# Softmax attention in a hybrid encoder block: sine products of the queries on GpSimd, half of the probabilities' products on ScalarE, and the values split during the linear attention

## The chip, the cores and the metric

The kernel runs on one core of one Trainium2 chip. The metric is device time in microseconds (us), the median of several executions. A core has five engines that run their own instruction lists in order and meet at semaphores: TensorE (PE in the profile: matmuls and transposes into PSUM), VectorE (DVE), ScalarE (ACT), GpSimd (POOL) and SyncE (SP), which in this kernel issues every DMA.

## The reference, cut to what matters

One encoder layer over 1024 tokens of width 1024: a projection of the normalized input, a gated linear attention (GLA), a softmax attention over a window of +-128 tokens (SWA), their gated sum, and a SwiGLU network. The part that the change touches is the softmax attention, with 8 query heads, 2 key/value heads, a head width of 128 and blocks of 128 tokens:

```python
def _rope(x, pos):
    ...
    x1, x2 = x[..., :half], x[..., half:]
    return jnp.concatenate([x1 * cos - x2 * sin, x2 * cos + x1 * sin], axis=-1)

def _swa_branch(q, k, v, q_g, k_g, sinks):
    ...
    q = _rope(_rms_norm(q.astype(f32).reshape(bsz, s, SWA_HEADS, hd), q_g), pos)
    k = _rope(_rms_norm(k.astype(f32).reshape(bsz, s, hkv, hd), k_g), pos)
    ...
    scores = jnp.einsum("bnqhgd,bnkhd->bnhgqk", qb, kc) * (hd ** -0.5)
    ...
    m = jnp.maximum(scores.max(axis=-1, keepdims=True), sink)
    p = jnp.exp(scores - m)
    denom = p.sum(axis=-1, keepdims=True) + jnp.exp(sink - m)
    o = jnp.einsum("bnhgqk,bnkhd->bnqhgd", p / denom, vc)
```

The probabilities, divided by their sum, multiply the values of up to three neighbouring blocks. All is float32.

## The kernel before, in words

Matrix products keep float32 accuracy by three passes: each operand is split into a rounded high part (type fp32r; names ending in h) and the remainder (names ending in l), and `mm3` runs high x high, high x low and low x high into the same PSUM tile. A weight unit of 128x512 is loaded by SP into one of 4 buffers `wr` (L68), rounded by ACT into `wh` (L70) and subtracted by DVE into `wl` (L72).

PE's order is written by hand: in the stages of the two attentions, `slot` calls small functions of the attention (called stages here) and, between them, `fill` takes dense matmuls (tiles `mm`) of the projections that are still due from the list `dense`. So while PE waits for an attention step it cannot reorder; a wait of PE there is lost unless a later wait becomes shorter by it. The other engines' orders are set by the scheduler that builds the program: it simulates the program with its own costs and lists each engine's instructions in the order in which they came to be ready there. It also gives out the buffers of pools in that order: the four PSUM banks for the attention's tiles (`ch`), and the SBUF buffers of each tag.

The GLA stage comes first (linear attention, functions `g_*`, 4 heads x 8 chunks of 128 tokens). For each chunk `g_scores` loads the split values `vh`, `vl` (3 buffers each in the pool `gt`), `g_out` reads them, and `g_turn` transposes the output (PE, L771), copies it with ACT into `ot` (L773) and stores it (L775, `o<-ot`). At the end of the stage stand 8 calls of `k_norm(t)`: each loads a block of keys of the softmax attention (`kvr`), normalizes and rotates it, and stores it to DRAM (`key`). They are called in the last slots, but all engines except PE run them as early as their data and buffers allow. The dense work beside the stage's end is the last of the projection to `sq1` (`proj_t`: PSUM tiles copied by ACT at L186, stored at L187, `sq<-st`) and the first of `r0`, `r1` (`proj_f`).

`glas.close()` frees the pools of the GLA stage. The buffers of the softmax attention (SWA) lie in the same memory, so its first loads (`cosb`, `sinb`, `band`, `qg`, `sink`) wait for the last users of those buffers. From these tables DVE builds `qA` and `qB` (L859 to L862), which hold the cosine and sine times the key-side gain.

The SWA stage treats 16 chunks: 2 groups g of 4 heads, by 8 blocks n of 128 queries. Chunk i is loaded (`a_load`) in slot i, prepared in slot i+1 (`a_prep`: `qr` squared by ACT, summed by DVE; the rotation is two products with `qB` at L912 and L914, one with `qA` at L916, and a sum at L917), transposed in slot i+2 (`a_turn`), scored in slot i+3 (`a_scores`: for each of four heads three matmuls into a `ch` bank, then DVE's row maximum `mx` at L941; behind the fourth head the maxima with the sink, four exponentials on ACT at L956, their sums `dn`, the reciprocal `rd` at L960 and four products of the probabilities `p` with `rd` on POOL at L962), and finished in slot i+5 (`a_probs`: PE transposes the probabilities by key block, ACT rounds them to `ph` at L976, DVE makes `pl` at L977; `a_out`: products with the split values). In the slots of the first 8 chunks `k_load(t)` loads a block of keys and of values, `k_turn` transposes the keys (`kTh`, `kTl`), and `k_prep` splits the values: `vSh` on ACT (L894), `vSl` on DVE (L895).

## Time and profile before

| | before |
|---|---|
| median of 3 runs | 1645.5 us (1644.73 to 1645.68) |
| the profiled execution, its own time | 1645.61 us |
| its span in the profile | 1643.8 us |
| granted TensorE clock in the span | 1.00 |
| busy in the span: PE, DVE, ACT, POOL | 1626.0, 1251.4, 842.6, 76.0 us |
| DMA moved | 262.91 MB |

Busy PE time is the union of the matmuls' modelled times, so it counts as busy what runs behind each other without a gap; PE's idle time is the span less that. Line numbers (L912) are those of the kernel before. A row of the timeline gives the start in us, the length in us, the engine, the line, the operation, the tiles as out<-in, the shapes and, in square brackets, how long the engine had been idle and what released it. SPq is SP's queue of DMA issues.

### The profile page before, as it was taken

What the parts mean: (1) busy time and instruction counts of PE and PEld (TensorE: products, weight loads), DVE (VectorE), ACT (ScalarE), POOL (GpSimd) and SP (SyncE); (2) the same over time, 40 slices, a digit from 0 to 9 for tenths busy, and PEclk for the clock granted to TensorE, in tenths of its full rate; (3) what the DMA queues carried; (4) which work ended last, traced back from release to release, by engine and by line L of the source; (5) the groups of instructions that cost most, each with busy time, mean ns of one, the idle gap of its engine ahead of it and who ended that gap; (6) DMA issues with size and microseconds to landing.
All of it is one profiled execution on the core that took longest, in us unless ns stands there. A gap on an engine that the chain in (4) does not pass through costs nothing.

```text
span 1643.8 us, 23281 instructions
## 1 busy us (share of the span) xinstructions
PE 1626.0 (99%) x7588; PEld 1346.0 (82%) x7588; DVE 1251.4 (76%) x2559; ACT 842.6 (51%) x1762; POOL 76.0 (5%) x68
## 2 busy tenths in 40 slices
PE   9999999999999989999999999999999999999999
PEld 7888888888888778888888888888888888888887
DVE  8866665589986598867885678887777778779655
ACT  8622224468998666665554557333333333354442
POOL 0000000000000034540000000000000000000000
PEclk9999999999999999999999999999999999999999
DMA  7554334475554633248765544443334443596433
GB/s 238 176 178 148 115 122 135 173 250 173 179 161 129 191 108 97 77 138 280 225 205 175 168 146 145 140 149 109 109 115 147 142 147 129 177 341 193 149 98 119
DMA packets 168010, 262.91 MB, mean 160 GB/s; under 512 B 19324, under 2 KB 52860, under 8 KB 167888
## 3 DMA queue, kind: packets, MB, share of 16 engines
q1 hardware_dynamic: 167888, 261.42, 49.8%
q8 instruction: 60, 0.98, 0.2%
q14 instruction: 62, 0.51, 0.1%
HBM read 187.93 MB, written 73.42 MB: 159 GB/s over the span
## 4 chain that ended last, share of the span: by engine, by line
PE 84%; DVE 9%; ACT 4%; DMA 2%; issue 1%; POOL 1%; SPq 0%; ACTq 0%; DVEq 0%
PE mm L76 23%; PE mm L306 9%; PE mm L308 9%; PE mm L307 9%; PE mm L1350 7%; PE ch L1350 5%; PE ch L76 4%; PE ch L306 4%; PE ch L308 4%; PE ch L307 4%; PE ch L460 3%; PE mm L460 2%; ACT p L956 1%; DVE wl L72 1%; DVE cs L655 1%
## 5 line engine op out<-in xcount | busy, mean ns | idle before, releaser
L298 ACT ACTIVATE wh<-ws 128x512 fp32r<-128x512 f32 x132 | 83.3, 632 | 195.9 <-PE mm L307 102.2
L70 ACT ACTIVATE wh<-wr 128x512 fp32r<-128x512 f32 x202 | 124.9, 626 | 87.4 <-PE mm L76 54.9
L72 DVE TENSOR_TENSOR wl<-wr,wh 128x512 fp32r<-128x512 f32 x202 | 137.7, 686 | 26.8 <-ACT wh L70 26.4
L299 DVE TENSOR_TENSOR wl<-ws,wh 128x512 fp32r<-128x512 f32 x132 | 90.5, 686 | 22.7 <-ACT wh L298 22.6
L298 ACT ACTIVATE wh<-wr 128x512 fp32r<-128x512 f32 x69 | 43.6, 632 | 124.8 <-issue 49.7
L962 POOL TENSOR_SCALAR p<-p,rd 128x384 f32<-128x384 f32 (+1 forms) x64 | 75.8, 1202 | 657.1 <-DMA qr<-sq 587.2
L298 ACT ACTIVATE wh<-a 128x512 fp32r<-128x512 f32 x64 | 40.5, 633 | 91.4 <-PE ch L1350 42.3
L76 PE MATMUL mm<-wh,xl 128*128 128x512 f32 x192 | 83.1, 433 | 0.0
L76 PE MATMUL mm<-wh,xh 128*128 128x512 f32 x192 | 79.6, 415 | 0.0
L76 PE MATMUL mm<-wl,xh 128*128 128x512 f32 x192 | 79.6, 414 | 0.0
L299 DVE TENSOR_TENSOR wl<-a,wh 128x512 fp32r<-128x512 f32 x64 | 44.2, 691 | 43.1 <-ACT wh L298 42.5
L1350 PE MATMUL mm<-hh,wh 128*128 128x512 f32 x176 | 68.5, 389 | 0.0
L1350 PE MATMUL mm<-hl,wh 128*128 128x512 f32 x176 | 68.5, 389 | 0.0
L1350 PE MATMUL mm<-hh,wl 128*128 128x512 f32 x176 | 68.5, 389 | 0.0
L76 PE MATMUL mm<-xl,wh 128*128 128x512 f32 x160 | 64.5, 403 | 0.1
L76 PE MATMUL mm<-xh,wh 128*128 128x512 f32 x160 | 64.4, 403 | 0.2 <-ACT wh L70 0.2
L76 PE MATMUL mm<-xh,wl 128*128 128x512 f32 x160 | 59.2, 409 | 0.0
L1320 DVE TENSOR_TENSOR hl<-hr,hh 128x512 fp32r<-128x512 f32 x75 | 51.4, 685 | 3.7 <-ACT hh L1319 3.7
L1350 PE MATMUL ch<-hh,wh 128*128 128x512 f32 x132 | 51.3, 389 | 0.0
L1350 PE MATMUL ch<-hl,wh 128*128 128x512 f32 x132 | 51.3, 389 | 0.0
L1350 PE MATMUL ch<-hh,wl 128*128 128x512 f32 x132 | 51.3, 389 | 0.0
L76 PE MATMUL mm<-oah,wh 128*128 128x512 f32 x128 | 50.2, 392 | 0.0
(620 smaller groups left out, 5077.7 us busy)
## 6 DMA issues: line engine op xcount, KB each, us to landing
wr<-in_w_fi_dram SPq DMA_DIRECT2D x102, 256.0 KB
wr<-in_w_f_dram SPq DMA_DIRECT2D x80, 256.0 KB
wr<-in_w_t_dram SPq DMA_DIRECT2D x56, 256.0 KB
B<-c SPq DMA_DIRECT2D x44, 256.0 KB
T<-tx SPq DMA_DIRECT2D x44, 256.0 KB
a<-in_w_fo_dram SPq DMA_DIRECT2D x44, 256.0 KB
hr<-T SPq DMA_DIRECT2D x44, 256.0 KB
wr<-in_w_ob_dram SPq DMA_DIRECT2D x32, 256.0 KB
```

The lines of the kernel that those rows point to most:

```text
L70: nc.scalar.activation(h, raw, AF.Copy)
L72: nc.vector.tensor_tensor(l, raw, h.bitcast(F32), op=ALU.subtract)
L76: nc.tensor.matmul(o, a, b, start=start, stop=stop)
L298: nc.scalar.activation(h, src, AF.Copy)
L299: nc.vector.tensor_tensor(l, src, h.bitcast(F32), op=ALU.subtract)
L306: nc.tensor.matmul(o, h[:, c], x[kk][0], start=start and kk == 0, stop=False, skip_group_check=True)
L307: nc.tensor.matmul(o, h[:, c], x[kk][1], start=False, stop=False, skip_group_check=True)
L308: nc.tensor.matmul(o, l[:, c], x[kk][0], start=False, stop=kk == nk - 1, skip_group_check=True)
L460: nc.tensor.matmul(ys[m], a[:, c], b, start=f0, stop=f1, skip_group_check=True)
L962: nc.gpsimd.tensor_scalar(p[:, h, :w], p[:, h, :w], rd[:, h:h + 1], None, op0=ALU.mult)
L1320: nc.vector.tensor_tensor(l, r, h.bitcast(F32), op=ALU.subtract)
L1350: nc.tensor.matmul(ys[m], a[:, c], b, start=f0, stop=f1, skip_group_check=True)
```

## The change

Three edits, all around the softmax attention.

1. The two products of the queries with the sine table (L912, L914) go from DVE to POOL. They write a tile `qb` of their own (2 buffers), and the square that ACT makes for the norm gets another (`sq`, 1 buffer), where both shared one tile before.
2. Of the four products of a chunk's probabilities with `rd`, those of heads 0 and 1 go from POOL to ACT (an activation Copy with a scale for each row); heads 2 and 3 stay on POOL.
3. The values are split in `k_norm`, in the GLA stage: SP loads them (`svr`, 2 buffers), POOL rounds them to `vh` and subtracts to `vl` (in the buffers of that tag which `g_scores` uses), and SP stores both to DRAM (`sh`, `sl`). `k_load` then loads `vSh` and `vSl` ready made, `k_prep` is gone, and so is its entry in the order of a slot.

```diff
@@ def k_norm(t)
             need(("skv", t))
-            raw = gtile("kvr", (P, 2, P))
+            raw, v = gtile("kvr", (P, 2, P)), gtile("svr")
             nc.sync.dma_start(out=raw.rearrange("p a b -> p (a b)"), in_=scr["skv", t][:, 0:256])
+            nc.sync.dma_start(out=v, in_=scr["skv", t][:, 256:512])
+            vh, vl = (gtile(nme, dt=FR, bufs=3) for nme in ("vh", "vl"))
+            nc.gpsimd.tensor_copy(vh, v)
+            nc.gpsimd.tensor_tensor(vl, v, vh.bitcast(F32), op=ALU.subtract)
+            for nme, u in (("sh", vh), ("sl", vl)):
+                scr[nme, t] = scratch(f"{nme}_{t}", (P, 256))
+                nc.sync.dma_start(out=scr[nme, t], in_=u.bitcast(F32))
@@ def k_load(t), def k_prep(t)
-            raws[t] = sw.tile([P, 256], F32, tag="kvr", name=nm("kvr"))
-            need(("skv", t))
-            nc.sync.dma_start(out=raws[t], in_=scr["skv", t][:, 256:512])
             keys[t] = sw.tile([P, 2, P], F32, tag="key", name=nm("key"))
             nc.sync.dma_start(out=keys[t].rearrange("p a b -> p (a b)"), in_=scr["key", t])
+            for nme, u in (("sh", vSh), ("sl", vSl)):
+                nc.sync.dma_start(out=u[t].bitcast(F32), in_=scr[nme, t])
...
-        def k_prep(t):
-            v2 = raws.pop(t)
-            nc.scalar.activation(vSh[t], v2, AF.Copy)
-            nc.vector.tensor_tensor(vSl[t], v2, vSh[t].bitcast(F32), op=ALU.subtract)
@@ def a_prep(g, n)
-            b = sw.tile([P, 4, P], F32, tag="sq4", name=nm("sq"))
-            a.rs = inv_norm(qr, 4, b, 1.0, EPS * 128, eps128)
+            b = sw.tile([P, 4, P], F32, tag="sq4", name=nm("qb"))
+            sq = sw.tile([P, 4, P], F32, tag="kvr", name=nm("sq"), bufs=1)
+            a.rs = inv_norm(qr, 4, sq, 1.0, EPS * 128, eps128)
             a.qn = sw.tile([P, 4, P], F32, tag="qn4", name=nm("qn"))
-            nc.vector.tensor_tensor(b[:, :, 0:64], qr[:, :, 64:128], qB[:, n:n + 1, 0:64].to_broadcast([P, 4, 64]),
+            nc.gpsimd.tensor_tensor(b[:, :, 0:64], qr[:, :, 64:128], qB[:, n:n + 1, 0:64].to_broadcast([P, 4, 64]),
                                     op=ALU.mult)
-            nc.vector.tensor_tensor(b[:, :, 64:128], qr[:, :, 0:64], qB[:, n:n + 1, 64:128].to_broadcast([P, 4, 64]),
+            nc.gpsimd.tensor_tensor(b[:, :, 64:128], qr[:, :, 0:64], qB[:, n:n + 1, 64:128].to_broadcast([P, 4, 64]),
                                     op=ALU.mult)
@@ def a_scores(g, n, h)
             for h in range(4):
-                nc.gpsimd.tensor_scalar(p[:, h, :w], p[:, h, :w], rd[:, h:h + 1], None, op0=ALU.mult)
+                if h < 2:
+                    nc.scalar.activation(p[:, h, :w], p[:, h, :w], AF.Copy, scale=rd[:, h:h + 1])
+                else:
+                    nc.gpsimd.tensor_scalar(p[:, h, :w], p[:, h, :w], rd[:, h:h + 1], None, op0=ALU.mult)
```

The scheduler lists the other engines' instructions anew. The first place is SP's list near the end of the GLA stage, before the change: weight units (`wr`), with the outputs of the GLA chunks (`o<-ot`) between them.

```order
L68 DMA wr_6739<-in_w_f_dram 128x512
L775 DMA o_0_3097<-ot_6313 128x128
L775 DMA o_0_3099<-ot_6313 128x128
L775 DMA o_0_3097<-ot_6322 128x128
L775 DMA o_0_3099<-ot_6322 128x128
L68 DMA wr_6745<-in_w_f_dram 128x512
L68 DMA wr_6800<-in_w_f_dram 128x512
```

With the change, the unit that was `wr_6800` (the first of `r1`) is called `wr_6880`. SP lists the value loads and stores in pairs of blocks; of the last two blocks these rows stand ahead of that unit (the GLA outputs of `ot_6603` and `ot_6618` are between them):

```order
L791 DMA sl_6657<-vl_6652 128x256
L785 DMA svr_6700<-skv_3927 128x256
L785 DMA svr_6782<-skv_3971 128x256
L775 DMA o_1_3102<-ot_6603 128x128
L775 DMA o_1_3104<-ot_6603 128x128
L775 DMA o_1_3102<-ot_6618 128x128
L775 DMA o_1_3104<-ot_6618 128x128
L791 DMA sh_6707<-vh_6703 128x256
L791 DMA sl_6709<-vl_6704 128x256
L791 DMA sh_6789<-vh_6785 128x256
L791 DMA sl_6791<-vl_6786 128x256
L68 DMA wr_6880<-in_w_f_dram 128x512
```

What moved is the unit: it stands behind value loads and stores that weren't there. The rows before these go in the same manner: the loads `svr` of blocks 2 and 3 stand behind the stores of blocks 0 and 1, those of blocks 4 and 5 behind the stores of 2 and 3, and those of blocks 6 and 7 (above) behind the stores of 4 and 5. Two weight units stand between the loads of blocks 2 and 3 and their stores, one behind the loads of 4 and 5, none behind those of 6 and 7. On ACT and PE the end of the GLA stage keeps its order.

The second place is DVE's list early in the SWA stage, where chunk 0 has been scored (`nm` is its negated maximum, `dn` and `rd` its sum and reciprocal) and chunk 1's first maxima `mx` follow. Before:

```order
L917 TENSOR_TENSOR qn_7186<-qn_7186,sq_7173 128x512
L958 TENSOR_TENSOR dn_7130<-dn_7130,es_7127 128x4
L102 TENSOR_TENSOR rt_7181<-rt_7181,rl_7178 128x4
L125 TENSOR_TENSOR st_7197<-mm_6984,rstd 128x512
L960 RECIPROCAL rd_7136<-dn_7130 128x4
L103 SCALAR_TENSOR_TENSOR rt_7181<-rt_7181,rl_7178 128x4
L72 TENSOR_TENSOR wl_7206<-wr_7202,wh_7204 128x512
L104 SCALAR_TENSOR_TENSOR rs_7177<-rt_7181,rl_7178 128x4
L941 ISA p_7209,mx_7210<-ch_7211,band 128x384
```

And with the change (L943 is the maximum, L960 and L962 are `dn` and `rd`):

```order
L943 ISA p_7265,mx_7266<-ch_7267,band 128x384
L943 ISA mx_7266 128x1
L103 SCALAR_TENSOR_TENSOR rt_7254<-rt_7254,rl_7251 128x4
L919 TENSOR_TENSOR qn_7259<-qn_7259,qb_7245 128x512
L104 SCALAR_TENSOR_TENSOR rs_7250<-rt_7254,rl_7251 128x4
L125 TENSOR_TENSOR st_7274<-mm_7060,rstd 128x512
L125 TENSOR_TENSOR st_7278<-mm_7061,rstd 128x512
L960 TENSOR_TENSOR dn_7204<-dn_7204,es_7201 128x4
L943 ISA p_7265,mx_7266<-ch_7290,band 128x384
```

The first maximum of chunk 1 moved ahead of chunk 0's sum.

The third place is ACT's list in the middle of the SWA stage, around three exponentials of chunk 4, the output copy `sob` of an earlier chunk, and the rounding `ph` of another chunk's transposed probabilities. Before:

```order
L956 ACTIVATE p_7755,dn_7787<-p_7755,nm_7780,rs_7452 128x384 x3
L987 COPY sob_7827<-ch_7817 128x512
L976 ACTIVATE ph_7849<-ch_7844 128x512
L976 ACTIVATE ph_7859<-ch_7854 128x512
L976 ACTIVATE ph_7869<-ch_7864 128x512
```

And with the change, where these lines are L958, L992 and L981, and the products are L965:

```order
L958 ACTIVATE p_7677,dn_7725<-p_7677,nm_7718,rs_7382 128x384 x3
L992 COPY sob_7765<-ch_7755 128x512
L965 ACTIVATE p_7677<-p_7677,rd_7731 128x384 x2
L981 ACTIVATE ph_7781<-ch_7776 128x512
L981 ACTIVATE ph_7791<-ch_7786 128x512
L981 ACTIVATE ph_7801<-ch_7796 128x512
```

The two products have come between the copy and the roundings. They stand ahead of all three `ph` of the slot for 6 of the 16 chunks (the 4th to 6th and the last three), between them or behind them for the others. On PE the order of the attention's matmuls is the same up to where the dense matmuls fall between them. The PSUM banks are given out anew: a score tile stands in the same bank as the score tile just before it in 9 slots, where it was 5 before.

More of the change, by code (lines that the diff above doesn't have):

```diff
@@ L1021, in body @@
                 todo[n + 1].append((k_turn, n))
-                todo[n].append((k_prep, n))
                 if n:
@@ L1025, in body @@
             todo[n].append((a_load, g, t))
-        order = (a_probs, k_prep, a_prep, a_scores, a_turn, k_turn, a_out, k_load, a_load)
+        order = (a_probs, a_prep, a_scores, a_turn, k_turn, a_out, k_load, a_load)
         k_load(0)
```

## The prediction

> **What bounds the kernel now.** I read the page's busy times first, then the busy times by stretch (stretch, length, then busy us of PE, PEld, DVE, ACT and POOL, clock, DMA share, GB/s), then who PE waited for between 565 and 620 us (total, times, longest).
>
> ```profile
> PE 1626.0 (99%) x7588; PEld 1346.0 (82%) x7588; DVE 1251.4 (76%) x2559; ACT 842.6 (51%) x1762; POOL 76.0 (5%) x68
> 500.00:565.00 65.00, 64.46 (x331) 53.40 (x330) 31.99 (x94) 49.05 (x146) 0.00 (x0) 1.00 0.49 152
> 565.00:620.00 55.00, 48.95 (x258) 40.07 (x258) 53.11 (x168) 35.46 (x97) 18.34 (x16) 1.00 0.45 136
> 620.00:740.00 120.00, 116.51 (x632) 97.66 (x631) 97.03 (x314) 80.56 (x208) 57.48 (x49) 1.00 0.33 102
> PE ch L923 <- DVE mx L941: 1.9, 1, 1.9
> PE ch L76 <- DVE pl L977: 1.0, 1, 1.0
> PE ch L973 <- POOL p L962: 0.9, 2, 0.6
> PE ch L76 <- DVE kTl L903: 0.6, 1, 0.6
> PE ch L923 <- DVE qn L917: 0.5, 1, 0.5
> ```
>
> PE is busy for 1626.0 of 1643.8 us, so the change, which takes no matmul away, can only remove PE's gaps. Where it works these are 0.54 us (65.00 - 64.46) up to 565, 6.05 us from 565 to 620, and 3.49 us from there to 740. So the most to win is 10.1 us. What PE loses, on the other hand, is nowhere got back, since it has no gaps behind this stage to speak of. In 565 to 620 DVE is busy for 53.11 of 55 us: it is the limit there, and one wait for it (1.9 us) is a third of the gap. From 620 on DVE has a fifth of its time free.
>
> **Part one: the start of the softmax stage.** DVE's rows around the long wait (start, length, engine, line; in brackets the idle time and what ended it), PE's wait itself, and the operations that leave DVE (times are min/median/max in ns):
>
> ```profile
> 586.24 0.16 DVE L958 TENSOR_TENSOR dn<-dn,es 128x4 f32<-128x4 f32 x1
> 587.31 0.69 DVE L72 TENSOR_TENSOR wl<-wr,wh 128x512 fp32r<-128x512 f32 x1
> 587.98 0.55 DVE L941 CUSTOM_DVE_ANT_0 p<-ch,band 128x384 f32<-128x384 f32 x1
> 588.60 0.66 PE L923 MATMUL ch<-ident,qn 128*128 128x128 f32 x4 [1.86 <-DVE mx L941]
> L912 DVE TENSOR_TENSOR sq<-qr,qB x16: 411/417/424, 570.3 to 688.7; 128x256 f32<-128x256 f32 x16
> L914 DVE TENSOR_TENSOR sq<-qr,qB x16: 409/418/422, 570.7 to 689.0; 128x256 f32<-128x256 f32 x16
> L895 DVE TENSOR_TENSOR vSl<-kvr,vSh x8: 412/416/418, 567.5 to 603.1; 128x256 fp32r<-128x256 f32 x8
> 572.56 0.66 PE L923 MATMUL ch<-ident,qn 128*128 128x128 f32 x4 [0.50 <-DVE qn L917]
> ```
>
> DVE loses 16 x (0.417 + 0.418) + 8 x 0.416 = 16.7 us in the stage. Up to 620 it loses the eight subtractions (3.3 us) and the products of about six chunks (6 x 0.835 = 5.0 us). Besides, the maximum of chunk 1, which started at 587.98 behind the sum `dn` (it had to wait for chunk 0's exponentials), now stands ahead of it. So the 1.9 us go. The 0.9 us for POOL's products go too: two of the four are now ACT's. Of the 0.6 us for `kTl` I take half. The waits for `pl` stay, as ACT's `ph` comes first there. That is 1.9 + 0.9 + 0.3 = **3.1 us less**, between 0 (if the next thing in each place is equally late) and all 6.05. The first transposition of queries waited 0.50 us for `qn`; its sum now stands on DVE behind one product in place of three, but also behind two on POOL: **0.3 less**, between -0.5 and +1.5 (two products of POOL's longest row, below, against two of DVE's).
>
> **Part two: the middle.** One slot of it on DVE and PE:
>
> ```profile
> 691.70 0.16 DVE L958 TENSOR_TENSOR dn<-dn,es 128x4 f32<-128x4 f32 x1 [2.25 <-ACT p L956]
> 692.02 0.56 DVE L941 CUSTOM_DVE_ANT_0 p<-ch,band 128x384 f32<-128x384 f32 x1
> 692.64 0.44 PE L76 MATMUL ch<-kTh,sqh 128*128 128x384 f32 x1 [0.54 <-DVE mx L941]
> ```
>
> DVE waited 2.25 us for the exponentials, so the products that go were no burden here. PE's 0.54 us is a round trip: a score tile in the same PSUM bank as the one ahead of it can't begin until DVE has taken the maximum of that one (0.56 us). A faster DVE list doesn't shorten it. Such neighbours are 9 now and were 5, which would cost 4 x 0.54 = 2.2 us if nothing else waited in those slots; but most slots lose half a microsecond to one wait or the other. I take **0**, between -2 and +2.2.
>
> What ACT and POOL gain in work, by these rows (the first two are groups: busy us, mean ns, then idle time):
>
> ```profile
> L962 POOL TENSOR_SCALAR p<-p,rd 128x384 f32<-128x384 f32 x48 | 59.8, 1263 | 57.6 <-DVE rd L960 22.0 <-ACT ph L976 14.7 <-ACT sob L987 8.2
> L962 POOL TENSOR_SCALAR p<-p,rd 128x256 f32<-128x256 f32 x16 | 16.1, 1020 | 599.5 <-DMA qr<-sq 587.2 <-DVE rd L960 5.8 <-ACT sob L987 3.5
> L962 POOL TENSOR_SCALAR p<-p,rd x64: 922/1247/1740, 587.6 to 732.4; 128x384 f32<-128x384 f32 x48, 128x256 f32<-128x256 f32 x16
> L894 ACT ACTIVATE vSh<-kvr x8: 401/412/420, 565.6 to 595.9; 128x256 fp32r<-128x256 f32 x8
> 551.58 0.69 ACT L186 ACTIVATE st<-mm,rstdt 128x512 f32<-128x512 f32 x1 [0.33 <-PE mm L76]
> ```
>
> ACT gets 24 products of 128x384 and 8 of 128x256, and loses 8 x 0.412 = 3.3 us. A product of 128x384 lies between 0.41 (the smaller rounding) and 0.69 (the larger scaling); I take the middle, 0.55, so 24 x 0.55 + 8 x 0.41 = 16.5 us, or 0.55 x 2 = 1.1 us in a chunk. ACT is idle for 39 of the 120 us to 740, which covers it where it isn't ahead of something that PE waits for: that is rival three. POOL keeps two products (2 x 1.26) and gets two of 128x256 with two inputs, an operation that no row shows on POOL. Nearest is its own 128x256 with one input, 1.02; below it is DVE's 0.42 for the same products, above it POOL's longest row, 1.74. At 1.02 a chunk takes POOL 4.6 us, where it took 4 x 1.26 = 5.0. So POOL doesn't bound the middle, even at 1.74 (6.0 us in a slot of about 10: POOL's 57.48 us in 120 are 11.5 chunks).
>
> **Part three: the end of the linear attention**, which decides the sign. Rows of SP's queue, then of the others, and one piece of the chain of waits (start, length, what):
>
> ```profile
> 527.16 0.38 SPq L187 DMA_DIRECT2D sq<-st  x1
> 534.42 1.90 SPq L68 DMA_DIRECT2D wr<-in_w_f_dram  x2
> 579.57 2.63 DMA qr<-sq
> 550.21 0.62 ACT L70 ACTIVATE wh<-wr 128x512 fp32r<-128x512 f32 x1
> 552.17 0.90 ACT L765 ACTIVATE ob<-ob,ors 128x256 f32<-128x256 f32 x2
> 554.31 0.69 ACT L186 ACTIVATE st<-mm,rstdt 128x512 f32<-128x512 f32 x1 [0.66 <-PE mm L76]
> 554.11 0.38 PE L771 MATMUL ch<-ident,ob 128*128 128x128 f32 x2
> 557.02 0.37 ACT ot L773
> 557.41 0.32 SPq L775
> 557.78 1.69 DMA o<-ot
> 559.67 0.33 SPq L63
> 560.05 0.42 SPq L63
> 561.46 3.58 DMA sink<-in_sink_dram
> 565.05 0.46 DVE qA L859
> ```
>
> The stage's entry is a chain: ACT's last `ot` copy (557.02), the store, its landing, the table loads one behind the other (0.47 us apart with the gaps), the landing of the last (3.58), then `qA`. Anything that makes the `ot` copy late makes the whole stage late, as PE's order is fixed.
>
> SP issues in order, and a store that waits for POOL holds up all that is behind it. The value blocks go in pairs with two buffers. Behind the `sq` store (527.16) three stores and two loads follow, so the loads of blocks 2 and 3 are out at 527.16 + 5 x 0.47 = 529.5. From there each pair takes a load's landing (2.63), four POOL operations (together S), and an issue (0.47), three times over, before the weight unit `wr_6880` is issued at X = 529.5 + 3 x (3.1 + S). Before, that unit was the second issued from 534.42. ACT rounds it at 550.21, and ACT too goes in order: behind it stand the scalings `ob` (552.17) that PE transposes at 554.11, and the `ot` copy. The unit lands at X + 2.6, and of ACT's lateness its idle 0.33 and about half of its 0.66 are taken up. So the entry is late by X + 2.6 - 550.2 - 0.7 = X - 548.3, that is 3S - 9.5. With S = 4 x 1.02 = 4.08: X = 551.0, and the entry is **2.7 us late**. The bounds of the operation give 0 (4 x 0.42 = 1.7: the unit is in time) and 3 x 6.96 - 9.5 = 11.4. At 1.02 the cover is gone by little: it holds up to S = 3.2.
>
> The other transfers cost SP's slots alone: eight value loads more in the first stage, sixteen stores, eight loads more in the second, at DMA shares of 0.33 to 0.49. PE uses `wr_6880` itself only behind the entry.
>
> The Trainium skill speaks to the operation in its "GPSIMD Engine Reference", section "3.1 Elementwise — side-by-side cycle accounting": a product of two tensors with 2048 elements in a row takes 4497 ns there. In proportion 256 elements would take 0.56 us (an estimate by that page), S would be 2.2, the entry in time, and the result that of rival one. The 1.02 us that the simpler operation took here speaks against going by proportion.
>
> **The sum**: 2.7 - 0.3 - 3.1 + 0 = -0.7. The profiled execution took 1645.6 us (1643.8 in its span), 0.1 above the median of the runs, which is within their spread. So 1645.6 - 0.7 = 1644.9, and beside the median 1644.8.
>
> **The rivals.**
>
> *One: the values are ready in time.* If S is below 3.2, POOL's chain ends before ACT asks for the unit, and the gain at the start is whole: 1645.5 - 3.4 = 1642.1, as low as 1640 if more of the 6.05 us goes. For it: DVE's 0.42, and that the last pair need not wait for a full landing. Against it: POOL's 1.02 for less work.
>
> *Two: the value chain makes the stage slower.* One mechanism, the one of part three, in the weight unit behind the value stores: from S = 5.4 (1.35 an operation) the lateness 3S - 9.5 is 6.7, which outweighs the gain of 3.4 by 3.3, that is 0.2%. At POOL's longest row, S = 6.96, it is 11.4 - 3.4 = +8.0: 1653.5. At casts of 1.2 and subtractions of 1.7, S = 5.8, it is +4.5: 1650.0. For it: two inputs are more work than one. Against it: most of POOL's rows are near 1.02 for this shape.
>
> *Three: ACT's products come ahead of `ph`.* In 6 chunks both stand ahead of all three roundings, 1.1 us each; if PE waits for 0.7 us of that in each, it is 4.2, and 1644.8 + 4.2 = 1649.0. Against it: half a microsecond of most slots is already lost beside it.
>
> *Four: the relief of DVE is given back.* The Trainium skill, "GPSIMD Engine Reference", section "1. Specifications at a glance", has it that GpSimd's SBUF interfaces are shared with VectorE, with contention where VectorE reads two inputs from SBUF. What speaks to it here:
>
> ```profile
> L916 DVE TENSOR_TENSOR qn<-qr,qA x16: 676/683/693, 568.7 to 695.9; 128x512 f32<-128x512 f32 x16
> ```
>
> A DVE product with two inputs took 676 to 693 ns, whether POOL worked or not, so nothing was shared with POOL's one-input products; no row shows POOL with two. If DVE were stretched by a fifth for the 16 x 2 x 1.02 = 33 us of these, it would be 6.5 us, and about half of the start's gain would go: 1646.3.
>
> **How the numbers follow.** About what a measurement of this kernel can tell from no change is 0.2%, 3.3 us: faster is below 1642.2, slower above 1648.8. The forecast's case, with S between 3.2 and 5.4, spans about 1642.2 to 1648.8 and has 0.45, since the nearest row lies in its middle. Rival one has 0.26, two 0.18, three 0.06, four 0.05. So faster 0.26, within 0.45 + 0.05 = 0.50, slower 0.18 + 0.06 = 0.24. The range takes 1640.5 (most of rival one) to 1651.0 (the nearer half of rival two).
>
> **What would show it.** In the profile after: the POOL rows of the values' rounding and subtraction (S); the issue of the unit behind the last `sl` store (551 by the forecast, and before 548 by rival one, past 555 by rival two); ACT's idle time ahead of that `wh`; the time of `qA` (565.1 + 2.7). PE's idle time in the 55 us from the entry should fall from 6.05 to about 2.6, the 1.86 us ahead of the transposition should be gone, and in the next 120 us it should stay at 3.5. I would be wrong if PE waits for something that I did not price, such as POOL's sine products ahead of its probabilities.

## The result, and the profile after

The changed kernel takes 1649.61 us, the median of 11 runs (1648.21 to 1651.0), against 1645.5 us (1644.26 to 1646.82): a ratio of 1.0025, 95% interval [1.0016, 1.0034]. It is 4.1 us slower, with an interval clear of no change, where 0.7 us less was forecast. The profiled execution has a span of 1647.8 us, 4.0 more than before.

Where the 4 us arise is seen by comparing the same matmul in two traces. A lag is the start of a matmul in one run less its start in the run before; from each lag the one at 530 us is taken off, since up to there the programs do the same, and the profiles differ by up to 0.4 us there. The columns are the time in the trace before: the end of the linear attention (550), the first transposition of queries (572.6), the start of the softmax stage passed (632), its last three chunks begun (710), the stage passed (750).

```
                 550    572.6   632     710     750
changed kernel  +1.05  +2.28   +1.67   +1.48   +4.01
```

So 1.05 us are lost in the linear attention, 1.2 at the entry, 0.6 are won back at the start of the softmax stage, and 2.5 go in the last 40 us of the stage. Behind it the lag stays (+3.8 at 1600).

The value split first. These are rows of the timeline of the changed kernel: GpSimd's subtractions, two small VectorE operations of the output norm, the PE transposition at the end of that chain, and SP's issue of the weight unit that the forecast was about.

```profile
545.78 0.74 POOL L788 TENSOR_TENSOR vl<-svr,vh 128x256 fp32r<-128x256 f32 x1
545.89 0.66 DVE L101 TENSOR_SCALAR rt<-oss 128x2 f32<-128x2 f32 x1 [0.64 <-ACT osq L760]
546.94 0.73 POOL L788 TENSOR_TENSOR vl<-svr,vh 128x256 fp32r<-128x256 f32 x1
546.97 0.72 DVE L103 SCALAR_TENSOR_TENSOR rt<-rt,rl 128x2 f32<-128x2 f32 x1
548.48 0.44 PE L771 MATMUL ch<-ident,ob 128*128 128x128 f32 x2 [0.49 <-ACT ob L765]
548.11 0.55 SPq L68 DMA_DIRECT2D wr<-in_w_f_dram  x1
```

The unit is issued at 548.11, and ScalarE rounds it at 551.80 without having waited for it. But two VectorE operations on two elements a row last 0.66 and 0.72 us: they end at 546.55 and 547.69, with GpSimd's subtractions (546.52, 547.67). They stand in the chain sum of squares, `ors`, scaling `ob`, transposition, and PE waits at its end (0.49 us here). The same operation over both kernels (min/median/max in ns; before, then after):

```profile
L101 DVE TENSOR_SCALAR rt<-oss x16: 159/169/171, 402.6 to 550.3; 128x2 f32<-128x2 f32 x16
```

```profile
L101 DVE TENSOR_SCALAR rt<-oss x16: 155/168/656, 402.8 to 551.6; 128x2 f32<-128x2 f32 x16
```

The median stands, the maximum is nearly four times as long. GpSimd's groups in the changed kernel (busy us, mean ns, idle time before):

```profile
L967 POOL TENSOR_SCALAR p<-p,rd 128x384 f32<-128x384 f32 x24 | 29.6, 1244 | 42.5 <-ACT ph L981 17.6 <-ACT sob L992 16.0 <-DVE rd L962 8.8
L916 POOL TENSOR_TENSOR qb<-qr,qB 128x256 f32<-128x256 f32 x16 | 12.7, 796 | 0.0
L788 POOL TENSOR_TENSOR vl<-svr,vh 128x256 fp32r<-128x256 f32 x8 | 6.4, 796 | 0.6
L787 POOL CAST vh<-svr 128x256 fp32r<-128x256 f32 x8 | 3.9, 487 | 536.5 <-PE ch L76 521.3 <-DMA svr<-skv 15.2
```

A rounding takes 0.49 and a subtraction 0.80 us on average, so the four of a pair are S = 2.6 us, where 4.08 was taken.

Then the entry. The first table load waits for the landing of the linear attention's last output store (a piece of the chain of waits, and SP's row):

```profile
559.05 2.33 DMA o<-ot
561.92 0.33 SPq L63 DMA_DIRECT2D cosb<-in_c_cos_dram  x1
```

That store landed 1.69 us after its issue before, 2.33 now, and from its issue to the table load it is 2.87 us where it was 1.89. In the rows of SP, two more weight loads (issued at 553.98 and 555.57) now stand in the 5 us ahead of it. So `qA` starts 1.95 us late (taken as the lags are), and the rest up to 2.28 goes with a longer wait for `qn`.

The start: PE's rows at the first transposition and at the one that waited 1.86 us before, `qA`, the sum `qn`, then PE's waits and the busy times from 567 us on.

```profile
567.16 0.69 DVE L866 TENSOR_TENSOR qA<-cosb,qg 128x512 f32<-128x512 f32 x1 [3.35 <-DMA key<-key]
574.30 0.69 DVE L919 TENSOR_TENSOR qn<-qn,qb 128x512 f32<-128x512 f32 x1 [0.71 <-POOL qb L916]
575.05 0.66 PE L925 MATMUL ch<-ident,qn 128*128 128x128 f32 x4 [1.62 <-DVE qn L919]
583.53 0.66 PE L925 MATMUL ch<-ident,qn 128*128 128x128 f32 x4 [0.41 <-DVE mx L943]
PE ch L76 <- DVE mx L943: 1.5, 2, 0.9
PE ch L76 <- DVE kTl L904: 1.3, 2, 0.9
PE ch L978 <- POOL p L967: 1.0, 2, 0.6
567.00:622.00 55.00, 48.78 (x256) 39.38 (x254) 50.72 (x152) 36.42 (x97) 23.29 (x26) 1.00 0.53 160
```

The wait of 1.86 us has shrunk to 0.41, as forecast. But waits for other maxima (0.5 before) are 1.5, for `kTl` 1.3 (0.6 before), and POOL's products still cost 1.0 (0.9 before). The sum `qn` now waits 0.71 us for GpSimd. PE idles 6.2 of 55 us, as it did. VectorE is still busy for 50.7 of them: operations of less than 0.25 us there last in sum 5.7 us longer than the shortest of their kind between 565 and 640 us, against 1.3 before (added up over the two traces).

Last, the stage's end. ACT's rows in one of the last slots before, the copy and the three roundings behind each other:

```profile
720.00 0.56 ACT L987 COPY sob<-ch 128x512 f32<-128x512 f32 x1
720.46 1.74 ACT L976 ACTIVATE ph<-ch 128x512 fp32r<-128x512 f32 x3
```

And ACT's, DVE's and PE's rows in the slots of the last chunks with the change:

```profile
723.52 0.56 ACT L992 COPY sob<-ch 128x512 f32<-128x512 f32 x1
724.12 1.12 ACT L965 ACTIVATE p<-p,rd 128x384 f32<-128x384 f32 x2
725.15 1.54 ACT L981 ACTIVATE ph<-ch 128x512 fp32r<-128x512 f32 x3
725.75 1.89 DVE L982 TENSOR_TENSOR pl<-ch,ph 128x512 fp32r<-128x512 f32 x3 [0.41 <-ACT ph L981]
727.55 0.42 DVE L943 CUSTOM_DVE_ANT_0 p<-ch,band 128x256 f32<-128x256 f32 x1
734.40 0.91 ACT L965 ACTIVATE p<-p,rd 128x256 f32<-128x256 f32 x2 [0.48 <-DVE rd L962]
735.21 1.55 ACT L981 ACTIVATE ph<-ch 128x512 fp32r<-128x512 f32 x3
735.84 0.50 PE L76 MATMUL ch<-ph,vSh 128*128 128x512 f32 x1 [0.53 <-ACT ph L981]
```

The two products (1.03 us, then 0.81) stand between the output copy and the roundings; `pl` comes later by that, DVE's maxima behind `pl` too. PE's waits that the profile puts to an engine between 700 and 746 us are 2.2 us, for `pl`, `mx`, `ph` and `sob`, against 1.2 us before; they don't account for all of the 2.5.

### The profile page after: what moved, and what is told of

Read it like the earlier page. It is cut to its first block, busy times and chain, and to the rows that moved or that the text cites. A ratio compares the mean times of both kernels' runs of the same rounds, so it can differ in the third digit from the quotient of the medians.

```text
span 1647.8 us, 23395 instructions
## 1 busy us (share of the span) xinstructions
PE 1627.6 (99%) x7588; PEld 1346.8 (82%) x7588; DVE 1244.6 (76%) x2519; ACT 854.9 (52%) x1786; POOL 73.5 (4%) x84
## 4 chain that ended last, share of the span: by engine, by line
PE 85%; DVE 8%; ACT 3%; issue 1%; DMA 1%; SPq 0%; POOL 0%; DVEq 0%; ACTq 0%
PE mm L76 23%; PE mm L306 9%; PE mm L307 9%; PE mm L308 9%; PE mm L1354 7%; PE ch L1354 5%; PE ch L76 5%; PE ch L307 4%; PE ch L306 4%; PE ch L308 4%; PE ch L460 3%; PE mm L460 2%; DVE wl L72 1%; DVE cs L655 1%; ACT p L958 1%
## 5 line engine op out<-in xcount | busy, mean ns | idle before, releaser
L72 DVE TENSOR_TENSOR wl<-wr,wh 128x512 fp32r<-128x512 f32 x202 | 137.6, 687 | 26.4 <-ACT wh L70 26.3
L76 PE MATMUL mm<-oal,wh 128*128 128x512 f32 x128 | 49.8, 389 | 0.0
```

The source lines that it names most:

```text
L72: nc.vector.tensor_tensor(l, raw, h.bitcast(F32), op=ALU.subtract)
L76: nc.tensor.matmul(o, a, b, start=start, stop=stop)
```

## The experiments

Three theories were tried: **lock** (GpSimd's operations hold up VectorE's), **queue** (value loads and stores in SP's list), **products** (ScalarE's products ahead of the roundings). All runs were timed in five rounds against the kernel before, which took 1645.6 to 1645.7 us in them.

### Each edit alone, and the change without edit 3

**Edit 1 alone** (a separate tile for the square, as in the change):

```diff
-            nc.vector.tensor_tensor(b[:, :, 0:64], qr[:, :, 64:128], qB...
-            nc.vector.tensor_tensor(b[:, :, 64:128], qr[:, :, 0:64], qB...
+            nc.gpsimd.tensor_tensor(b[:, :, 0:64], qr[:, :, 64:128], qB...
+            nc.gpsimd.tensor_tensor(b[:, :, 64:128], qr[:, :, 0:64], qB...
```

> The kernel before with edit 1 alone (sine products on GpSimd). Three theories on the 4.1 us: lock (a two-input GpSimd operation holds up VectorE's small operations and stretches them), queue (the value loads and stores in SP's list make the entry of the softmax stage late), products (ScalarE's products ahead of the roundings at the stage's end). All expect no change up to the entry (lag under 0.3 us at 550 and at the first transposition of queries, but for the wait for GpSimd's products there). Queue and products: the relief of VectorE shows whole, 1 to 2 us faster than before. Lock: VectorE's small operations from 570 to 740 last about 4 us longer in sum, and the time is within 1 us of before.

**Edit 2 alone**:

```diff
+                if h < 2:
+                    nc.scalar.activation(p[:, h, :w], p[:, h, :w], AF.Copy, scale=rd[:, h:h + 1])
+                else:
+                    nc.gpsimd.tensor_scalar(p[:, h, :w], p[:, h, :w], rd[:, h:h + 1], None, op0=ALU.mult)
```

> The kernel before with edit 2 alone (products of heads 0 and 1 on ScalarE). Products: no lag up to 700 us, then 2 to 3 us in the last three chunks (710 to 740), where the two products stand ahead of all three roundings, so 2 to 3 us slower. Lock and queue: nothing there, and 0 to 1 us faster, as the two waits for GpSimd's products at the start go.

**Edit 3 alone** (`k_norm` and `k_load` as in the change, edits 1 and 2 undone):

```diff
+            nc.gpsimd.tensor_copy(vh, v)
+            nc.gpsimd.tensor_tensor(vl, v, vh.bitcast(F32), op=ALU.subtract)
...
+            for nme, u in (("sh", vSh), ("sl", vSl)):
+                nc.sync.dma_start(out=u[t].bitcast(F32), in_=scr[nme, t])
```

> The kernel before with edit 3 alone (values split in the linear attention). Lock: PE is 0.7 to 1.2 us late already at 550, before any value load of the softmax stage, with VectorE operations of the linear attention stretched while GpSimd subtracts. Queue: nothing at 550, but the first load of queries is issued about 1 us or more later after the last output store, and the first transposition is 1 to 2.5 us late. Products: neither. VectorE's eight subtractions less give back at most 3 us of it by 620; so between 1 us faster and 2 us slower than before.

**Edits 1 and 2 without 3** (`k_norm`, `k_load` and `k_prep` as before):

```diff
-            nc.gpsimd.tensor_copy(vh, v)
-            nc.gpsimd.tensor_tensor(vl, v, vh.bitcast(F32), op=ALU.subtract)
...
+            nc.scalar.activation(vSh[t], v2, AF.Copy)
+            nc.vector.tensor_tensor(vSl[t], v2, vSh[t].bitcast(F32), op=ALU.subtract)
```

> The changed kernel without edit 3 (edits 1 and 2 on the kernel before). Lock and queue: the lag up to the first transposition of queries goes (under 0.7 us in place of 2.5). Products: the 2 to 3 us at 710 to 740 stay. If both hold, the time is 1 to 2 us below the changed kernel.

Measured (median us; ratio to before with its interval; lags as above):

```
                 us       ratio                     550    632     710     750
edit 1 alone     1651.64  1.0036 [1.0024, 1.0049]  +0.01  +1.90   +5.11   +4.81
edit 2 alone     1647.7   1.0016 [1.0007, 1.0025]  -0.01  -1.71   -1.39   +2.03
edit 3 alone     1650.0   1.0028 [1.0018, 1.0039]  +1.24  +4.55   +4.73   +4.42
edits 1 and 2    1649.09  1.0020 [1.0012, 1.0029]  +0.02  -0.19   +0.28   +3.00
```

Edit 2 alone is 2.1 us slower, inside the 2 to 3 that products expected, but by other parts: it wins 1.4 us up to 710, where no lag was expected, and then loses 3.4. Edit 1 alone was worse than lock expected (within 1 us of before): VectorE's operations of less than 0.25 us last 8.2 us longer in sum than before between 565 and 745 us, where about 4 was expected. PE's longest waits there, from 565 to 745 us:

```profile
PE ch L974 <- POOL p L963: 4.0, 6, 1.1
PE ch L76 <- DVE mx L942: 3.3, 5, 0.8
PE ch L76 <- DVE kTl L903: 2.3, 2, 1.3
```

With all four products and the sine products on GpSimd, the probabilities come late: 4.0 us, on top of VectorE's waits. Edit 3 alone is 1.24 us late at 550, as lock expected and queue didn't. At the first transposition it is 1.98 us late, which is in queue's range, and in the end it is beyond both: between 565 and 640 us PE waits 3.2 us for POOL's products there, and from 605.8 to 609.2 us, just after such a wait, the profile shows a granted TensorE clock of 0.50, which is about 1.7 us more (half of 3.4, an estimate). The run without edit 3 has no lag at the first transposition (-0.6 us) and loses 2.7 us behind 710, both as expected, yet it is only 0.5 us below the changed kernel, where 1 to 2 were expected.

So the edits are not additive: alone they cost 6.0, 2.1 and 4.4 us, together 4.1. That edit 2 takes from GpSimd what the others make wait fits PE's waits (its wait for POOL's products is 4.0 and 3.2 us in the runs without it, 1.0 with it), but wasn't tested by itself. Edit 1 on top of edit 2 costs 1.4 us.

### The last three chunks

```diff
-                if h < 2:
+                if h < 2 and (g, n) < (1, 5):
```

> The changed kernel, with all four products of the last three chunks on GpSimd again (the other chunks as in the change). Products: the lag of 1.7 us at 710 stays up to the end of the stage, and the 2.5 us behind it go: about 1647.1 us, 1.5 us above the kernel before. If that loss comes from the PSUM banks given out anew or from the entry, it stays, and the time is 1649.6.

Measured: 1646.53 us, ratio 1.0007 [0.9998, 1.0016]. From 710 to 750 the lag goes from -0.05 to -0.17 us, where the changed kernel's rose by 2.5. That is ScalarE's products there, with what the scheduler lists anew on VectorE behind them; all lists ahead of these chunks stay as they are. In this run's ACT rows the roundings follow the copy directly:

```profile
719.94 0.56 ACT L992 COPY sob<-ch 128x512 f32<-128x512 f32 x1
720.41 1.75 ACT L981 ACTIVATE ph<-ch 128x512 fp32r<-128x512 f32 x3
```

It shows one thing more: up to 713 us every engine's list is the changed kernel's, and it is 1.02 us late at the first transposition, against 2.28. So two executions of the same instructions differ by 1.2 us there. That isn't the size of what the change costs at the entry: the profiled execution of this run is the fastest of its eleven (1645.17 us, median 1646.53), that of the changed kernel is its median. And one part of the entry's lag comes back: from the issue of the last output store to the first table load it takes 2.53 to 3.12 us in all four profiles with the split on GpSimd (this run, the change, edit 3 alone, and the late value loads below), and 1.88 to 1.90 us in all ten others, the values on ScalarE and VectorE with their stores among them. So 0.6 to 1.2 us at the entry go with how SP's list falls with that split; which of its rows does it wasn't tried.

### The values without GpSimd, and GpSimd without the values

The changed kernel with the split on ScalarE and VectorE:

```diff
-            nc.gpsimd.tensor_copy(vh, v)
-            nc.gpsimd.tensor_tensor(vl, v, vh.bitcast(F32), op=ALU.subtract)
+            nc.scalar.activation(vh, v, AF.Copy)
+            nc.vector.tensor_tensor(vl, v, vh.bitcast(F32), op=ALU.subtract)
```

> The changed kernel, with the values rounded by ScalarE and subtracted by VectorE in the linear attention; loads, stores and edits 1 and 2 stay. Lock: no VectorE operation is stretched up to 560, and PE's lag at 550 is under 0.4 us in place of 1.1 (unless VectorE's own eight subtractions, 0.42 us each, fall into the same chain); the entry's lag shrinks by that. Queue: the lag at 550 stays, as SP's list still holds the value stores. By the lock alone the time falls by about 0.7 to 1.1 us.

The kernel before with GpSimd operations added, whose result isn't used (for the second run the last line is `nc.gpsimd.memset(d1, 0.0)`):

```diff
             nc.scalar.activation(sq, a.ob, AF.Square, accum_out=ss[:, 1 - c % 2:2 - c % 2])
+            if hd == NH - 1:
...
+                nc.gpsimd.tensor_tensor(d1[:, 0:1], a.ob[:, 0:1], a.ob[:, 0:1], op=ALU.mult)
+                nc.gpsimd.tensor_tensor(d1, d0, d0, op=ALU.mult)
```

> The kernel before, with eight GpSimd products of 128x256 with two inputs added, one behind each output chunk of the last head in the linear attention (their result isn't used; each starts when that chunk's sum is ready). Lock: VectorE's small operations of the norm's chain (0.16 us) last up to 0.7 us, PE's lag at 550 is 0.7 to 3 us, and the time rises by about that. Queue and products: nothing, as no transfer and no ScalarE work is added: within 0.3 us of before.

> The same kernel, with the eight products replaced by as many fills of 128x256 on GpSimd, which write and read nothing. If it is GpSimd's reading that holds up VectorE's operations with two inputs, the lag at 550 is under 0.3 us and the time within 0.5 us of before; if any GpSimd operation does, VectorE's small operations are stretched here too, by as long as a fill takes.

```
                      us       ratio                     550    632     710     750
values on ACT, DVE    1648.77  1.0018 [1.0009, 1.0027]  +0.23  +0.12   +0.32   +3.65
products added        1646.83  1.0007 [0.9998, 1.0016]  +0.90  +1.68   +1.66   +1.34
fills added           1645.64  1.0003 [0.9994, 1.0012]  +0.10  +0.12   +0.17   -0.14
```

Without GpSimd the value split costs 0.23 us at 550 in place of 1.05, with the value stores still in SP's list, and the time falls by 0.8. (The four profiles with the split on GpSimd have 1.05, 1.24, 1.03 and, with the late value loads below, 0.43 at 550.) Eight products added to the kernel before cost 0.90 there, with no transfer. As many fills cost 0.10. The pairs of rows, GpSimd's operation and the VectorE operation that starts in it, of the run with products:

```profile
534.07 0.61 POOL L767 TENSOR_TENSOR dm<-dm 128x256 f32<-128x256 f32 x1
534.24 0.47 DVE L101 TENSOR_SCALAR rt<-oss 128x2 f32<-128x2 f32 x1 [0.58 <-ACT osq L760]
```

and of the run with fills:

```profile
534.46 0.31 POOL L767 MEMSET dm<- 128x256 f32 x1
534.64 0.17 DVE L101 TENSOR_SCALAR rt<-oss 128x2 f32<-128x2 f32 x1 [0.58 <-ACT osq L760]
```

Both start inside GpSimd's operation. The one ends with the product (534.71 and 534.68), the other takes its usual 0.17. So a product of GpSimd holds up VectorE's operation until it ends. That a fill holds nothing isn't shown: it ends at 534.77 and VectorE's operation at 534.81, which is what a held one would do too, and the other pairs of this run don't tell either: VectorE's operation starts too near the fill's end, or with the fill, where a product (at 541.70) didn't hold one either. What the fills show is that it isn't the added GpSimd instructions as such, or what they wait for, that cost the 0.90.

The whole time of the run with products rose by 1.2 us with an interval that touches no change, so it is the rows and the lag at 550 that show the cause, not the median. Its lag at 632 has another part: from 589.4 to 592.9 us its profile shows a granted clock of 0.51, again just behind a long wait of PE (1.91 us). Queue is not needed for the lag at 550.

### Edit 2 without its end, and the lock in the softmax stage

Edit 2 on the kernel before, for the first 13 chunks:

```diff
+                if h < 2 and (g, n) < (1, 5):
+                    nc.scalar.activation(p[:, h, :w], p[:, h, :w], AF.Copy, scale=rd[:, h:h + 1])
```

> The kernel before with edit 2 for the first 13 of the 16 chunks alone (no edit 1, no edit 3). Products: the lag of edit 2 alone, -1.3 us at 710, lasts to the end, so about 1644.3 us, 1.3 us faster than before (0.3 to 2). If edit 2 costs something in any place, no faster than before.

The same with the sine products made a second time on GpSimd:

```diff
+            for k, j in ((0, 64), (64, 0)):
+                nc.gpsimd.tensor_tensor(dq[:, :, k:k + 64], qr[:, :, j:j + 64],
+                                        qB[:, n:n + 1, k:k + 64].to_broadcast([P, 4, 64]), op=ALU.mult)
```

> The same, with the two sine products of each chunk made a second time on GpSimd (their result isn't used; VectorE still makes its own). Lock: VectorE's small operations in 565 to 740 last 3 to 5 us longer in sum than in the run without them, and the time rises by 0.5 to 2.5 us. If edit 1 costs only because the rotation waits for GpSimd's result, or because the probabilities' products queue behind it, then with half of those products on ScalarE the rise is under 0.5 us.

The first took 1645.06 us, ratio 0.9994 [0.9986, 1.0003]: 0.6 us less, inside the expected range, half of the value named, and not clear of no change. It is 2.6 us below edit 2 in all chunks, so here too the last three are what costs. The second took 1651.34, ratio 1.0028 [1.0018, 1.0039], with a lag of +5.77 at 710 against -0.61: 6.3 us by the medians for work whose result nobody uses, where 0.5 to 2.5 were expected. Groups of VectorE from 565 to 745 us, without the added products:

```profile
L916 DVE TENSOR_TENSOR qn<-qr,qA 128x512 f32<-128x512 f32 x16 | 10.9, 684 | 0.0
L101 DVE TENSOR_SCALAR rt<-ss 128x4 f32<-128x4 f32 x16 | 2.6, 163 | 0.1
```

and with them (L916 is L920 there):

```profile
L920 DVE TENSOR_TENSOR qn<-qr,qA 128x512 f32<-128x512 f32 x16 | 13.1, 819 | 0.0
L101 DVE TENSOR_SCALAR rt<-ss 128x4 f32<-128x4 f32 x16 | 4.5, 284 | 0.1
```

The wide product lost 2.2 us and the small operation 1.9 over 16 chunks; all of VectorE's operations of less than 0.25 us last 5.6 us longer in sum than without the added products, where 3 to 5 were expected. PE's waits grow where VectorE is the limit (without the added products, then with them):

```profile
PE ch L923 <- DVE mx L941: 1.9, 1, 1.9
PE ch L923 <- DVE qn L917: 1.0, 1, 1.0
PE ch L927 <- DVE mx L945: 2.7, 1, 2.7
PE ch L927 <- DVE qn L921: 2.1, 1, 2.1
```

In sum PE's waits rise from 9.0 to 12.3 us between 565 and 745. None of them is for GpSimd, so the probabilities behind the added products are not what it waits for. The rest of the lag is the clock: the profile shows it granted in half for two stretches of 3.4 us, each behind one of the two longer waits (stretch, length, busy times, then clock, DMA share and GB/s):

```profile
574.80:578.20 3.40, 3.40 (x10) 2.71 (x9) 3.21 (x10) 2.48 (x7) 1.75 (x2) 0.50 0.67 198
591.90:595.30 3.40, 3.40 (x12) 2.83 (x12) 3.10 (x14) 1.07 (x3) 2.30 (x4) 0.50 0.44 153
```

That is about 3.4 us (half of 6.8, an estimate). So the lock's waits are about 3 us here, and the halved clock adds about as much. This run keeps the sine products on VectorE as well, so it bounds what the lock takes of edit 1 and doesn't measure it.

### The order of the loads, and a version that is faster

The changed kernel with the products of the last three chunks on GpSimd, and the value loads in a function of their own, called behind `a_load` one slot later:

```diff
+        def v_load(t):
             for nme, u in (("sh", vSh), ("sl", vSl)):
...
+                todo[n + 1].append((v_load, n))
```

> The changed kernel with the products of the last three chunks on GpSimd, and the loads of the split values behind the loads of queries in SP's list (two loads ahead of the first queries in place of six). Queue: the first load of queries is issued 1.9 us earlier after the last table load, PE's wait at the first transposition shrinks by 0.5 us or more, and the time falls by 0.3 to 1.2 us against the run with those products on GpSimd alone (1646.5). If the landing of the tables sets the entry, nothing changes.

Measured: 1646.22 us, ratio 1.0001 [0.9992, 1.0010], 0.3 us below the run without that (1646.53), which the scatter doesn't tell from nothing. The first load of queries is issued 1.9 us earlier behind the last table load (1.44 us in place of 3.34) and PE's wait for `qn` at the first transposition (0.77 us) is gone, both as queue has it, but a wait for the landing of keys (1.3 us) stands in its place. So the order of the value loads moves the wait and hardly the time.

Edits 2 and 3 with what had been learned: 13 chunks, no sine products on GpSimd, values split by ScalarE and VectorE, loads behind the queries':

```diff
-                if h < 2:
+                if h < 2 and (g, n) < (1, 5):
...
-            nc.gpsimd.tensor_copy(vh, v)
-            nc.gpsimd.tensor_tensor(vl, v, vh.bitcast(F32), op=ALU.subtract)
+            nc.scalar.activation(vh, v, AF.Copy)
+            nc.vector.tensor_tensor(vl, v, vh.bitcast(F32), op=ALU.subtract)
...
-            nc.gpsimd.tensor_tensor(b[:, :, 0:64], qr[:, :, 64:128], qB...
+            nc.vector.tensor_tensor(b[:, :, 0:64], qr[:, :, 64:128], qB...
```

> Edits 2 and 3 without what the other runs found to cost: products on ScalarE for the first 13 chunks, sine products on VectorE, values rounded by ScalarE and subtracted by VectorE in the linear attention, their loads behind the queries'. By lock, queue and products together nothing is left of the loss, and VectorE has eight subtractions less at the start: 1.3 to 3 us faster than before, at or below the run with edit 2 in 13 chunks alone. If the moved subtractions cost as much in the linear attention, or the entry is late anyway, no better than that run.

Measured: 1643.45 us, ratio 0.9987 [0.9978, 0.9996], 2.2 us faster than before and 6.2 faster than the change. Its lag is -2.70 at 632 and -2.51 at 750. PE's busy time from 565 to 620 us rose from 48.95 to 51.30:

```profile
565.00:620.00 55.00, 51.30 (x270) 42.22 (x270) 52.23 (x173) 37.03 (x101) 9.49 (x8) 1.00 0.52 160
```

That is 1.6 us below the run with edit 2 in 13 chunks alone. So moving the value split pays, if it is put where VectorE has room (32 of 65 us busy) and not on GpSimd; how much of it is due to the eight subtractions and how much to the order of the loads wasn't told apart.

## Why the prediction was wrong, point by point

**Part three, the entry.** Entry and first transposition were put at 2.7 - 0.3 = +2.4, and the lag there was +2.28, but not by the chain that was worked out; that the numbers are close is luck. S was 2.6, the weight unit was out at 548.11 and ACT didn't wait for it: that half went as rival one had it. The lag came from costs that had no term: VectorE's small operations behind GpSimd's subtractions, 1.05 us by 550, and 0.98 us more between the last output store and the first table load. The wait for `qn`, of which 0.3 us was to go, grew from 0.50 to 1.62 us.

**Part one, the start.** This is a step that failed: "3.1 us less". The 1.9 us did shrink to 0.41, yet the lag fell by 0.6 only, and PE's idle time in the 55 us, which was to fall to about 2.6, stayed at 6.2. Edit 2 alone gains 1.7 by 632; with edit 1 on top, 1.5 of it is gone. The 0.9 us for POOL's products, which were to go, stayed. The mechanism was rival four, given 5% and 1.5 us. It was read off the wrong row. Eight of the sixteen L916 ran beside one of GpSimd's products before, and all began 0.4 us or more behind its start, when the hold was over or nearly so. The rows of VectorE's small operations in the trace of before (min/median/max in ns) had it, and beside the second the rows of its longest, with GpSimd's product:

```profile
L952 DVE TENSOR_TENSOR es<-sink,mx x16: 149/156/472, 583.0 to 725.8; 128x4 f32<-128x4 f32 x16
L948 DVE TENSOR_TENSOR mx<-mx,rs x16: 146/156/445, 582.1 to 725.3; 128x4 f32<-128x4 f32 x16
706.14 1.25 POOL L962 TENSOR_SCALAR p<-p,rd 128x384 f32<-128x384 f32 x1
706.29 0.45 DVE L948 TENSOR_TENSOR mx<-mx,rs 128x4 f32<-128x4 f32 x1
```

An operation of 156 ns that takes 472 once is one that waited. The Trainium skill has the rule on another page than the one weighed, "SBUF — State Buffer", section "Who interferes with whom": a VectorE instruction with two SBUF inputs contends with a GpSimd instruction that reads SBUF, and the port pair that they share is an exclusive lock, which the one that issues first has for the whole instruction. The pairs of rows with two-input products agree: the held operation ends within 0.03 us of GpSimd's. The rows just shown don't agree with the last part: L948 is held until 706.74, 0.60 us behind the start of a product that lasts until 707.39. Here the measurement decides: a product with one tensor and a factor for each row held VectorE for the first 0.60 of its 1.25 us only. That a GpSimd instruction which only writes doesn't hold such an operation, as the Trainium skill's section has it too, no run here shows.

**Part two, the middle and the end.** "I take 0" is the other step that failed: it held up to 710 (-0.2 us) and not behind it (+2.5). PE's idle time in the 120 us behind the start, which was to stay at 3.5, was 5.2 us. The mechanism was rival three, ScalarE's products ahead of `ph`, given 6%. Its price was set at 0.7 us for each of six chunks; in the changed kernel's profile the lag doesn't rise over the three early ones, and by 2.5 us over the last three. That the cover ("half a microsecond of most slots is lost beside it") is gone because the stage's last slots hold less other work is an inference; that the loss comes with these products is shown.

**The sum.** Forecast 2.4 (entry and first transposition) - 3.1 + 0 = -0.7; found 2.3 - 0.6 - 0.2 + 2.5 = +4.0 in the profile. Two terms were wrong in size, both by mechanisms that stood among the rivals, and the entry's came out near by another way.

**The sizes of operations.** A product or difference of two tensors on GpSimd took 0.61 us (a contiguous tile times itself) to 0.74 us undisturbed. The estimate worked out from the Trainium skill ("GPSIMD Engine Reference", section "3.1 Elementwise — side-by-side cycle accounting") was 0.56, the size taken 1.02. ScalarE's product of 128x384 was put at 0.55; its pair lasted 1.12 us. Neither size decided the outcome.

## What to carry to other kernels

Work that is given to GpSimd is not taken off VectorE in full: beside GpSimd's products VectorE's operations wait (0.16 us became up to 0.72 here), and it is the smallest ones, in the chains that others wait for, that lose most. Look in the trace of before at the maximum beside the median of VectorE's shortest operations, before trusting a wide one. And work put on an engine with idle time costs by its place in that engine's list: ask at the ends of a stage, where the slots hold less, what stands behind it.

## What the runs showed of the hardware that was not expected

- A GpSimd product with two inputs of 128x256 (0.61 us) held VectorE's 0.17 us operation for 0.47. The operation held, L101, has one tensor input and two constants, so not only those with two inputs are held. VectorE's sum L752, with one input in SBUF and one in PSUM, wasn't: in the changed kernel it ran from 540.99 to 541.41 inside a subtraction that lasted until 541.73.
- How long the hold lasts depends on GpSimd's operation. With two tensor inputs it lasted to the end. In GpSimd's one-input products of 1.25 us before, eight small VectorE operations that began 0.15 to 0.38 us behind the start all ended 0.60 us behind it, and those that began 0.45 us or more behind it took 0.15 to 0.17 us, but for two near its end (0.18 and 0.25).
- It works the other way too: of two subtractions on GpSimd in the changed kernel, one alone took 0.73 us, and one that began beside VectorE's L72 (533.11 to 533.99) took 1.06. The prediction's row of POOL's longest operation shows the same: it lasted 1.74 us in place of 1.25, from 695.94, and VectorE's L916 ran from 695.87 to 696.56.
- The granted TensorE clock was halved for about 3.4 us, from less than 1 us behind the end of a wait of PE, in four places: behind waits of 1.33 us (edit 3 alone, after another of 0.75), 1.91 us (products added), and 2.05 and 2.73 us (edit 2 for 13 chunks, with added products). Behind waits of 1.86 us (before) and 1.90 us (edit 2 for 13 chunks) it wasn't, so no bound is shown, nor that the wait is the cause.
- The first transposition of queries came 1.02 us late in one execution and 2.28 in another of programs that are alike up to there.
